# Two banks of the last layer's modulation computed on VectorE from transposed weights, ahead of the recurrence instead of inside it

## The chip, the cores and the metric

The kernel runs on one core of a Trainium2 chip, in fp32, as one program. The metric is the device time of one execution in microseconds; of several runs the median is taken.

## What is computed

The reference chains two blocks over 256 tokens (and 256 context tokens) of 1024 features. The second block has two layers: an even mixer (latent attention and a convolution) and an odd mixer (an RWKV recurrence and neighbourhood attention), each followed by a mixture of 16 experts. Each layer is steered by a vector of 6 x 1024 modulations, computed from one conditioning row `c`:

```python
def second_block(x, c, ctx, c_ctx, ada_w, ada_b, ...):
    for i in range(DEPTH):                       # DEPTH = 2
        mod = jnp.einsum('bd,de->be', jax.nn.silu(c), ada_w[i]) + ada_b[i]   # 1024 x 6144 weights
        mod_c = jax.nn.silu(c_ctx) @ ada_w[i] + ada_b[i]
        sh1, sc1, g1, sh2, sc2, g2 = jnp.split(mod[:, None, :], 6, -1)
        h = rms_norm_2(x, norm1_g[i]) * (1.0 + sc1) + sh1
        ...
        y, yc = odd_mixer(h, hc, ...)            # i = 1: u = h @ w_in, then the recurrence
        x = x + g1 * y
        h = rms_norm_2(x, norm2_g[i]) * (1.0 + sc2) + sh2
        x = x + g2 * expert_choice_ffn(h, ...)
```

For the last layer only `mod` of `c` is used after the first norm (the context's columns count only in `sh1` and `sc1`).

## The kernel before

The program runs stage after stage; engines overlap within a stage and at its edges, in the order in which the program was scheduled. The stages that matter here, with their start in the trace: the first layer's experts (to about 1861 us); `odd_in` (1861 to 2034 us), which norms the tokens, multiplies them by the odd mixer's input weights `od_w_in` and prepares the recurrence; `rwkv` (2034 to 2268 us); the rest of the odd mixer (to 2345 us); the second layer's experts (to the end).

**The products of `odd_in`.** `features` norms and transposes the tokens and splits them into a high and a low part (`ah`, `al`; `al` is written by DVE, L364). A block of 1 MB of `od_w_in` is loaded by the SP queue (L380) into the tile `w`, of which there are three; its two halves are split likewise, `wh` by ACT (L347) and `wl` by DVE (L350), and a `w` is free again when both halves are split. A product is three matmuls (`wh` by `ah`, `wl` by `ah`, `wh` by `al`) for each of eight parts of the depth. `by_features` makes blocks of transposed products: `lwa`, `k`, `sgs` (the values) with 512 columns, `r` and `lg` with 256; each block is evacuated by one ACT and two DVE instructions (L1739, L1741), which shift and add. Then `lengths` norms the keys (a sum on PE, a RECIPROCAL on DVE at L1803, four products with `kk` at L1808), the values are transposed, `low_rank` runs, and the loop over `NO` makes the neighbourhood attention's queries, keys and values from three more sets of weights (`by_pairs`, `by_tokens`). `rwkv` comes behind all that: its first instruction on PE is a product into `py`.

**The modulations.** They are computed in three banks of 2048 columns by a generator, `mods_steps`. One step handles 128 rows of the weights: four loads of 256 KB (`mw`, L550) or one of 1 MB, and four fp32 matmuls with `silu(c)` as the 128x32 stationary operand. `want(m, bank)` allows a bank to be computed, `fill(n)` runs n steps wherever the code calls it, and `need(m, bank)` runs all steps that are still missing. The last layer's bank 0 is computed much earlier. Banks 1 and 2 are handed out inside `rwkv`, two steps at a time (`OF = (2, 2, 2)`): 64 loads `mw` into five buffers and 64 matmuls into `pd` (128 records in the trace, since an fp32 matmul is recorded as two). At the end of a bank the sums are transposed, the bias is added, and for the two gates a row is written out to memory. `by_features`, `by_pairs` and `by_tokens` call `fill(self.rate)` at their end, which in `odd_in` of the kernel before has nothing to run.

**Behind the modulations in `rwkv`.** The recurrence begins with four head pairs b = 0 to 3 (products into `py` and `pg` on PE, exponentials on ACT, products on DVE and POOL). Their triangular blocks `Lx` and `Lc` go to memory (`scr`, L2001) and come back turned round (`fsx<-scr`, L2004) for the substitution, a long run of small DVE instructions (L2018, L2020). The DMAs of both are issued by SP, as are the loads `mw`.

Of the kernel before, what the change touches and what calls it, by code (L numbers as in the profile page):

```python
# [9 lines left out]
F32 = mybir.dt.float32  # L10
# [4 lines left out]
AF = mybir.ActivationFunctionType  # L15
OP = mybir.AluOpType
# [3 lines left out]
D = 1024  # L20
# [65 lines left out]
def lay_out(inp):  # L86
    g = {k: np.asarray(v) for k, v in inp.items()}
    arrays = {}
# [24 lines left out]
    for name in ("w_mod", "ada_w_2", "diff_lambda",  # L113
# [5 lines left out]
    arrays["ctx_2"] = np.ascontiguousarray(g["ctx_2"][0])  # L119
    arrays["xT"] = np.ascontiguousarray(np.concatenate([g["x"][0].T, g["ctx"][0].T], 1).reshape(  # L120
        2, 4, 128, 512).transpose(0, 2, 1, 3))
    arrays["router"] = np.ascontiguousarray(
        g["moe_router_2"].reshape(2, 8, 128, 16).transpose(2, 0, 1, 3).reshape(128, 256))

# [5 lines left out]
    bias = np.full((8, T, T), -1e30, np.float32)  # L130
# [3 lines left out]
    col, qk = Pack(), []  # L134
# [47 lines left out]
    row, colm = (tok // 64).astype(np.float64), (tok % 64).astype(np.float64)  # L182
# [16 lines left out]
    cs = np.cos(2 * np.pi * (np.outer(tok, tok) % T) / T) / 16  # L199
# [18 lines left out]
    p = np.arange(128)  # L218
# [30 lines left out]
class Kernel:  # L249
# [245 lines left out]

    def mods(self, w, l, b, cx, cc, name):

        m = dict(name=name, done=-1, limit=-1)
        m["row"] = [self.dram.tile([2, D], F32, name=f"modr{name}{i}") for i in range(2)]
        self.fillers.append((m, self.mods_steps(m, w[l], f"{b}{l}", cx, cc)))  # L500
        return m

    def mods_steps(self, m, w, b, cx, cc):
        nc = self.nc
        for c in ("col", "col1"):
            m[c] = self.keep.tile([128, 12, 4, 2], F32, name=f"mod{c}{m['name'][1]}", bufs=1)
        sl = self.small.tile([128, KT, 32], F32, name="sil", bufs=1)
        nc.vector.memset(sl, 0.0)
        for v, cn in enumerate((cx, cc)):
            o, n = self.col_at[cn]  # L510
            nc.scalar.activation(sl[:, :, v], self.cols[:, o:o + n], AF.Silu)
        o, _ = self.col_at[b]
        for bank in range(3):
            ps = self.psum(self.modtag)
            for k in range(KT):
                ws = self.mod_weights(w[k * 128:(k + 1) * 128, bank * 2048:(bank + 1) * 2048])
                for g in range(4):
                    self.mm(ps[32 * g:32 * g + 32, :], sl[:, k, :], ws[g] if self.modpool else ws[:, g * 512:(g + 1) * 512],
                            k == 0, k == KT - 1)
                if k < KT - 1:  # L520
                    yield
            mr = self.small.tile([128, 512], F32, name="modrow", bufs=1)
            nc.scalar.copy(mr, ps)
            pt = self.psum()
            for s in range(4):
                self.transpose(pt[:, s * 128:(s + 1) * 128], mr[:, s * 128:(s + 1) * 128])
            v = pt.rearrange("p (s g r) -> p s g r", s=4, g=4)
            cs = slice(bank * 4, bank * 4 + 4)
            bias = self.cols[:, o + 16 * bank:o + 16 * bank + 16].rearrange("p (s g) -> p s g", s=4)
            c = m["col"][:, cs]  # L530
            nc.vector.tensor_tensor(c, v[:, :, :, 0:2], bias[:, :, :, None].to_broadcast([128, 4, 4, 2]), OP.add)
            nc.vector.tensor_scalar(m["col1"][:, cs], c, 1.0, None, OP.add)
            for sec, bk, g0 in ((0, 1, 0), (1, 2, 2)):
                if bk == bank:
                    gc = self.small.tile([128, 2, 2, 4], F32, name="gatec", bufs=1)
                    nc.vector.tensor_copy(gc, c[:, :, g0:g0 + 2].rearrange("p s g v -> p v g s"))
                    pt = self.psum()[:16, :128]
                    self.transpose(pt, gc.rearrange("p v g s -> p (v g s)"))
                    mr = self.small.tile([128, 512], F32, name="modrow", bufs=1)[:16, :128]
                    nc.scalar.copy(mr, pt)  # L540
                    nc.scalar.dma_start(m["row"][sec].rearrange("v (k f) -> (v k) f", f=128), mr)
            m["done"] = bank
            yield

    def mod_weights(self, src):

        if self.modpool:
            ws = [self.modpool() for _ in range(4)]
            for g, wt in enumerate(ws):
                self.nc.sync.dma_start(wt, src[:, g * 512:(g + 1) * 512])  # L550
            return ws
        wt = self.raw((1, 2048))[:, 0]
        self.last_load = self.nc.sync.dma_start(wt, src)
        return wt
# [53 lines left out]
class Block1(Kernel):  # L608
# [77 lines left out]
    def block1(self, mods):  # L686
        with self.pool("w4", "right") as self.fourth:
            self.need(mods[0], 0)
            for l in range(2):
                self.layer1(l, mods[l])  # L690
        self.fourth = None
# [961 lines left out]
class Odd(Moe):  # L1653
# [55 lines left out]
    def odd_in(self, m, od):  # L1709

        nc, a = self.nc, self.a
        W = lambda c0: a["od_w_in_2"][0, c0]
        with self.dense():
            self.need(m, 0)
            tmp = self.tmp
            self.wide = WIDE
            G = self.affine(m, "n1g1", 1, "G1")
            ah = tmp.tile([128, KT, 512], F32R, name="ah", bufs=1)
# [50 lines left out]
            self.nv = od.tile([128, 4, 512], F32, name="nv", bufs=1)  # L1769
            gain = self.small.tile([128, 1], F32, name="nag", bufs=1)  # L1770
            nc.vector.tensor_scalar(gain, self.col("nag", 0), self.col("nag", 1), 0.125, OP.mult, OP.mult)
            for c0, n, dT in NO:
                if dT is None:
                    self.by_tokens(self.halves(a["od_w_in_2"], c0), ahs, als, range(4),
                                   lambda tb, ps: nc.scalar.copy(self.nv[:, tb], ps))
                    continue
                dT = self.nkT if n == 4 else self.nqT
                for j in range(2):
                    z = tmp.tile([128, 4, 256], F32, name="nz", bufs=2)[:, :n]
                    self.by_pairs(W(c0 + j * 256), ahs, als, range(n // 2),  # L1780
                                   lambda tp, ps: nc.scalar.copy(z[:, tp * 2:tp * 2 + 2], ps))
                    self.head_norm(z.rearrange("p t (h d) -> p (t h) d", h=4), 64)
                    for i in range(2):
                        ps = self.psum()
                        for tb in range(n):
                            self.transpose(ps[:, tb * 128:(tb + 1) * 128], z[:, tb, i * 128:(i + 1) * 128])
                        nc.scalar.activation(dT[:, 2 * j + i], ps[:, :n * 128], AF.Copy, scale=gain if n == 2 else 1.0)
# [487 lines left out]
```

## Time and profile before

| | us |
|---|---|
| median of 3 runs | 2809.76 (2806.86 to 2818.59) |
| profiled execution | 2814.77 |
| its span in the trace | 2813.0 |

| engine | busy us | share of the span |
|---|---|---|
| PE (matmul) | 2558.9 | 91% |
| DVE | 1184.1 | 42% |
| ACT | 771.4 | 27% |
| POOL | 303.9 | 11% |

The shares are averages over stages with different limits, so they tell little of one change. In the two expert stages the DMA engines run at 407 to 421 GB/s and set the pace; in the stages between them PE, DVE or a chain over several engines does. The mean granted clock of TensorE over the run is 0.96 of full speed.

### The profile page before, as it was taken

How to read it: one execution, taken by the hardware profiler on the slowest of the kernel's cores; microseconds unless marked ns; L12 is line 12 of the kernel's file. 1: busy time of each engine (PE TensorE's matmuls, PEld its weight loads, DVE VectorE, ACT ScalarE, POOL GpSimd, SP SyncE). 2: the span in 40 equal slices, each digit the busy share in tenths (PEclk: the TensorE clock that was granted, in tenths of full speed). 3: DMA queues.
4: the chain of work that ended last, by engine and by line, in shares of the span. 5: the costliest groups of instructions: out<-in, count | busy, mean ns of one | idle time of the engine just before them, and what ended most of it. 6: DMA issues, size and time to landing. Idle time of an engine off the chain costs nothing.

```text
span 2813.0 us, 34600 instructions
## 1 busy us (share of the span) xinstructions
PE 2558.9 (91%) x13867; PEld 1564.3 (56%) x13867; DVE 1184.1 (42%) x2273; ACT 771.4 (27%) x1394; POOL 303.9 (11%) x370
## 2 busy tenths in 40 slices
PE   7999899997998998989899999989996897888887
PEld 4667688885766796757633333348644684222121
DVE  3355633347456467997511111155449452000000
ACT  3242322223343343276410000033442432000000
POOL 0001400004102003300100000000023130000000
PEclk8999999998998999999999999999998998999999
DMA  7443623223456854242699999953185548999998
GB/s 307 150 165 119 225 90 105 90 101 126 161 199 252 301 181 173 70 169 81 262 404 421 421 421 421 421 229 110 37 243 135 162 169 350 415 421 421 421 421 347
DMA packets 147216, 683.42 MB, mean 243 GB/s; under 512 B 38384, under 2 KB 51568, under 8 KB 71920
## 3 DMA queue, kind: packets, MB, share of 16 engines
q1 hardware_dynamic: 140656, 663.91, 61.6%
q10 hardware_dynamic: 6400, 17.31, 2.0%
q8 instruction: 109, 1.79, 0.3%
q14 instruction: 51, 0.42, 0.0%
HBM read 667.73 MB, written 11.60 MB: 241 GB/s over the span
## 4 chain that ended last, share of the span: by engine, by line
PE 51%; DMA 26%; DVE 8%; issue 2%; ACT 2%; POOL 0%; SPq 0%; ACTq 0%; DVEq 0%; POOLq 0%
DMA w<-in_moe_w 24%; PE pd L327 19%; PE pS L327 12%; PE pt L327 6%; PE pu L327 5%; PE ps L327 2%; PE pg L327 2%; PE pm L327 2%; DVE al L364 1%; PE ps L472 1%; PE pt L472 1%; PE pO L327 1%; DVE fs L2018 1%; DVE co L1152 1%; PE py L327 1%
## 5 line engine op out<-in xcount | busy, mean ns | idle before, releaser
L327 PE MATMUL pu<-w,xs 128*64 128x512 f32 (+1 forms) x2040 | 494.4, 599 | 42.9 <-DMA w<-in_moe_w 42.9
L350 DVE TENSOR_TENSOR wl<-w,wh 128x1024 fp32r<-128x1024 f32 x229 | 285.4, 1249 | 346.4 <-ACT wh L347 345.8
L347 ACT CAST wh<-w 128x1024 fp32r<-128x1024 f32 x250 | 259.7, 1041 | 598.5 <-PE pd L327 272.8
L327 PEld LDWEIGHTS pu<-w,xs 128*64 128x64 f32 (+1 forms) x2040 | 149.6, 123 | 370.7 <-issue 255.2
L327 PE MATMUL pd<-w,hidT 128*64 128x512 f32 (+1 forms) x1024 | 253.6, 598 | 31.0 <-DMA w<-in_moe_w 30.2
L327 PE MATMUL pd<-ah,wh 128*128 128x512 f32 (+2 forms) x656 | 233.6, 361 | 7.8 <-ACT wh L347 3.5
L327 PE MATMUL pd<-al,wh 128*128 128x512 f32 (+2 forms) x656 | 232.1, 355 | 8.6 <-DVE al L364 8.6
L327 PE MATMUL pd<-ah,wl 128*128 128x512 f32 (+1 forms) x648 | 227.1, 352 | 0.0
L1606 DVE TENSOR_TENSOR hid<-hid,pu 128x512 f32<-128x512 f32 x24 | 16.5, 688 | 439.3 <-PE pu L327 439.3
L1605 ACT ACTIVATE hid<-pu 128x512 f32<-128x512 f32 x24 | 14.2, 597 | 677.5 <-PE pu L327 677.5
L327 PEld LDWEIGHTS pd<-w,hidT 128*64 128x64 f32 (+1 forms) x1024 | 74.8, 122 | 200.2 <-issue 116.0
L327 PEld LDWEIGHTS pd<-ah,wh 128*128 128x128 f32 (+1 forms) x656 | 127.8, 196 | 42.6 <-issue 15.8
L327 PEld LDWEIGHTS pd<-al,wh 128*128 128x128 f32 (+1 forms) x656 | 128.6, 196 | 30.0 <-DVE al L364 10.5
L327 PE MATMUL pm<-w,sil 128*32 128x512 f32 x640 | 105.3, 697 | 41.9 <-DMA w<-in_w_mod 26.3
L327 PEld LDWEIGHTS pd<-ah,wl 128*128 128x128 f32 x648 | 126.9, 196 | 22.6 <-issue 8.2
L1615 DVE TENSOR_TENSOR ys<-pd,g 128x512 f32<-128x512 f32 x24 | 16.6, 692 | 285.0 <-PE pd L327 285.0
L1152 DVE SCALAR_TENSOR_TENSOR co<-cv,cols,co 128x512 f32<-128x512 f32 x120 | 100.5, 862 | 0.4
L1625 DVE TENSOR_TENSOR X<-X,ps 128x512 f32<-128x512 f32 x80 | 54.8, 687 | 107.2 <-PE ps L327 107.2
L327 PE MATMUL pS<-al,wh 128*128 128x256 f32 (+1 forms) x264 | 90.0, 342 | 5.0 <-DVE al L364 5.0
L327 PE MATMUL pS<-ah,wh 128*128 128x256 f32 (+1 forms) x264 | 89.8, 341 | 1.4 <-ACT ah L363 1.3
L327 PE MATMUL pS<-ah,wl 128*128 128x256 f32 (+1 forms) x264 | 89.3, 338 | 0.0
L327 PE MATMUL ps<-ys,gt 128*128 128x512 f32 x160 | 81.9, 625 | 2.1 <-DVE X L1625 2.1
(593 smaller groups left out, 4416.0 us busy)
## 6 DMA issues: line engine op xcount, KB each, us to landing
w<-in_moe_w SPq DMA_DIRECT2D x383, 1024.0 KB, 19.8
w<-in_w_mod SPq DMA_DIRECT2D x48, 1024.0 KB, 5.1
w<-in_w_up SPq DMA_DIRECT2D x32, 1024.0 KB, 4.9
w<-in_w_down SPq DMA_DIRECT2D x32, 1024.0 KB, 4.9
w<-in_ada_w SPq DMA_DIRECT2D x32, 1024.0 KB, 5.0
w<-in_w_in SPq DMA_DIRECT2D x20, 1024.0 KB, 4.9
mw<-in_ada_w SPq DMA_DIRECT2D x64, 256.0 KB, 3.9
w<-in_od_w_in SPq DMA_DIRECT2D x13, 1024.0 KB, 4.9
```

Of the source, the lines that this page charges most:

```text
L327: ins = self.nc.tensor.matmul(out, lhsT, rhs, start=start, stop=stop, skip_group_check=True)
L347: nc.scalar.copy(h, src)
L350: (le or nc.vector).tensor_tensor(l, src, h.bitcast(F32), OP.subtract)
L364: nc.vector.tensor_tensor(l, t, h.bitcast(F32), OP.subtract)
L472: ins = self.nc.tensor.transpose(out, in_, self.ident[:rows, :rows])
L1152: nc.vector.scalar_tensor_tensor(y, CV[:, f, :, t:t + T], self.col(f"dw{t}", f), y, OP.mult, OP.add)
L1605: nc.scalar.activation(hid[:, cs], up["moe_w1_2"][c], AF.Silu)
L1606: nc.vector.tensor_tensor(hid[:, cs], hid[:, cs], up["moe_w3_2"][c], OP.mult)
L1615: nc.vector.tensor_tensor(ys[:, cs], down[c], gate[:, cs], OP.mult)
L1625: nc.vector.tensor_tensor(self.X[tb][:, cs], self.X[tb][:, cs], ps, OP.add)
L2018: nc.vector.tensor_tensor(t, LM[:, s, tr, None].to_broadcast([128, nt_, nj]), X[:, s, None, jr].to_broadcast([128, nt_, nj]), OP.mult)
```

## The change

Banks 1 and 2 of the last layer no longer go to PE. `odd_in` gives the modulations room (a tile `sx` for the row `silu(c)`, broadcast to 128 partitions) and allows bank 2; every `fill` at the end of a step in `odd_in` then runs one step of a new generator, `mods_by_dve`. A step loads 1 MB of weights that were transposed on the host (`modT`) into the ring `w` of the input products, and runs two DVE instructions (128x1024, a pair in what follows) that multiply by `sx` and sum along the row into one column of `modacc`. A bank has eight steps. `need(m, 2)` just ahead of the loop over `NO` runs what is left. The order of the additions changes, the values computed do not.

```diff
+    arrays["modT"] = ... w[1][:, 2048:].T ... reshape(2, 4, 2, 2, 128, 1024).transpose(0, 1, 2, 4, 3, 5)
+    arrays["crow"] = np.stack([g[n].reshape(-1) for n in ("c", "c_2")])
@@ mods_steps
         for bank in range(3):
+            if m["room"] is not None and bank:
+                yield from self.mods_by_dve(m, bank, o)
+                continue
             ps = self.psum(self.modtag)
@@
+    def mods_by_dve(self, m, bank, o):
+        nc = self.nc
+        pair = "ma".index(m["name"][0])
+        if bank == 1:
+            m["sx"] = m["room"]()
+            nc.scalar.dma_start(m["sx"], self.a["crow"][pair:pair + 1].to_broadcast([128, D]))
+            nc.scalar.activation(m["sx"], m["sx"], AF.Silu)
+        cs = slice(bank * 4, bank * 4 + 4)
+        c = m["col"][:, cs]
+        nc.gpsimd.memset(c, 0.0)
+        acc = self.small.tile([128, 4, 4], F32, name="modacc", bufs=1)
+        for g in range(4):
+            for h in range(2):
+                wt = self.raw((2, 1024))
+                self.last_load = nc.sync.dma_start(wt, self.a["modT"][pair, bank - 1, g, h])
+                for i in range(2):
+                    nc.vector.scalar_tensor_tensor(wt[:, i], wt[:, i], 1.0, m["sx"], OP.mult, OP.mult,
+                                                   accum_out=acc[:, 2 * h + i, g:g + 1])
+                if g + h < 4:
+                    yield
+        bias = self.cols[:, o + 16 * bank:o + 16 * bank + 16].rearrange("p (s g) -> p s g", s=4)
+        nc.vector.tensor_tensor(c[:, :, :, 0], acc, bias, OP.add)
+        nc.vector.tensor_scalar(m["col1"][:, cs], c, 1.0, None, OP.add)
+        self.gate_rows(m, bank, c)          # the gate's row, as before
+        m["done"] = bank
+        yield
@@ odd_in
             tmp = self.tmp
+            m["room"] = lambda: tmp.tile([128, D], F32, name="sx", bufs=1)
+            self.want(m, 2)
@@
+            self.need(m, 2)
             for c0, n, dT in NO:
```

The program is scheduled anew, so the order on the engines moves too. Lines of the kernel after stand higher than the same lines before: L575 is the new DVE instruction, L573 its load, L355 the split L350, L385 the load L380, L1666 the sum L1625, L489 to L494 the steps L484 to L489.

DVE, at the end of the first layer's experts (`X`) and the start of `features` (`rsw`, `xrs`: the norm's reciprocal root), before:

```order
L1625 TENSOR_TENSOR X_74<-X_74,ps 128x512 x2
L484 TENSOR_SCALAR rsw<-ss 128x1
L485 TENSOR_SCALAR xrs<-rsw 128x1
L488 TENSOR_SCALAR rsw<-xrs,rsw 128x1
L489 TENSOR_SCALAR xrs<-rsw,xrs 128x1
```

and after:

```order
L1666 TENSOR_TENSOR X_74<-X_74,ps 128x512 x2
L575 SCALAR_TENSOR_TENSOR w,modacc<-w,sx 128x1024 x2
L489 TENSOR_SCALAR rsw<-ss 128x1 x2
L575 SCALAR_TENSOR_TENSOR w,modacc<-w,sx 128x1024 x2
L490 TENSOR_SCALAR xrs<-rsw 128x1 x2
L493 TENSOR_SCALAR rsw<-xrs,rsw 128x1 x2
L494 TENSOR_SCALAR xrs<-rsw,xrs 128x1 x2
```

Two pairs now stand ahead of the norm that every input product waits for; a third stands 29 rows below the second, between the two scalings `nk<-X` of the same stage.

DVE, from the last block of `by_features` (`lg`) over `lengths` to the first weights of `NO` (the `wl` behind `kk`), before:

```order
L350 TENSOR_TENSOR wl<-w,wh 128x1024
L1739 SCALAR_TENSOR_TENSOR lg<-pS,cols,lg 128x255
L1741 SCALAR_TENSOR_TENSOR lg<-pS,cols,lg 128x255
L1802 TENSOR_SCALAR tf<-ps 8x512
L1803 RECIPROCAL tf<-tf 8x512
L1808 TENSOR_TENSOR kk<-kk,ps 128x512 x2
L350 TENSOR_TENSOR wl<-w,wh 128x1024
```

and after:

```order
L1782 SCALAR_TENSOR_TENSOR lg<-pS,cols,lg 128x255
L575 SCALAR_TENSOR_TENSOR w,modacc<-w,sx 128x1024 x2
L1784 SCALAR_TENSOR_TENSOR lg<-pS,cols,lg 128x255
L1846 TENSOR_SCALAR tf<-ps 8x512
L575 SCALAR_TENSOR_TENSOR w,modacc<-w,sx 128x1024 x2
L1847 RECIPROCAL tf<-tf 8x512
L575 SCALAR_TENSOR_TENSOR w,modacc<-w,sx 128x1024 x6
L1852 TENSOR_TENSOR kk<-kk,ps 128x512 x2
L575 SCALAR_TENSOR_TENSOR w,modacc<-w,sx 128x1024 x2
L1852 TENSOR_TENSOR kk<-kk,ps 128x512
L580 TENSOR_TENSOR modcol_9263<-modacc,cols 128x16
L355 TENSOR_TENSOR wl<-w,wh 128x1024
```

Six of bank 2's eight pairs stand here, ahead of the first weights of `NO` (the last `wl` shown); the other two stand 2 and 6 rows ahead of the first row shown. In the kernel before three `wl` of `NO` stand ahead of the `lg` rows, of which the first row shown is the third.

SP, the loads of the input weights up to `NO` (the last but one of `by_features`, the last, then six of `NO`) and the recurrence's first DMAs, before:

```order
L380 DMA w<-in_od_w_in 128x1024
L380 DMA w<-in_od_w_in 128x2048 x6
L550 DMA mw<-in_ada_w 128x512 x19
L1978 DMA sp_13924<-MV 128x4x128
L1989 DMA sp_13924<-zt 64x4x128 x2
L550 DMA mw<-in_ada_w 128x512 x2
```

and after:

```order
L573 DMA w<-in_modT 128x2048
L385 DMA w<-in_od_w_in 128x1024
L573 DMA w<-in_modT 128x2048 x9
L385 DMA w<-in_od_w_in 128x2048 x6
L1885 DMA nbias<-in_na_bias 128x512
L2022 DMA sp_14013<-MV 128x4x128
L2033 DMA sp_14013<-zt 64x4x128 x4
```

All loads of the transposed weights stand ahead of the first load of `NO`, and all of them share the three tiles `w`; the recurrence's own DMAs no longer have loads `mw` between them. The first load of `NO` takes the tile that the third pair from the last has read, and the two loads behind it those of the last two pairs.

## Rows read from the trace of the kernel before

**Rows 1.** Engines by stage, whole core (x: instructions; PEclk: granted clock).

```profile
core 0: us, PE busy (x) PEld busy (x) DVE busy (x) ACT busy (x) POOL busy (x), PEclk, DMA share, GB/s
...
1860.00:1890.00 30.00, 22.43 (x90) 16.89 (x89) 18.70 (x62) 14.61 (x33) 0.00 (x0) 0.77 0.29 107
1890.00:1947.00 57.00, 57.00 (x308) 49.27 (x308) 36.40 (x46) 24.14 (x33) 0.00 (x0) 1.00 0.35 122
1947.00:2033.00 86.00, 79.61 (x456) 61.63 (x453) 40.15 (x80) 37.63 (x58) 2.38 (x3) 0.97 0.16 55
2033.00:2060.00 27.00, 25.05 (x247) 11.74 (x248) 13.79 (x21) 11.12 (x32) 10.88 (x12) 0.89 0.61 183
2060.00:2090.00 30.00, 30.00 (x223) 11.06 (x222) 15.32 (x28) 15.43 (x33) 6.81 (x9) 1.00 0.79 227
2090.00:2130.00 40.00, 31.91 (x325) 14.89 (x324) 28.40 (x57) 17.75 (x51) 19.87 (x20) 1.00 0.71 214
2130.00:2180.00 50.00, 29.71 (x520) 23.92 (x521) 47.15 (x126) 9.02 (x19) 9.63 (x8) 0.73 0.58 128
```

**Rows 2.** Stage table for instructions touching tile `mw` alone.

```profile
2033.00:2060.00 27.00, 13.76 (x39) 2.03 (x40) 0.89 0.61 183
2060.00:2090.00 30.00, 14.06 (x42) 1.85 (x41) 1.00 0.79 227
```

**Rows 3.** Tile `mw`, its SP loads (issue time min/median/max).

```profile
L550 SPq DMA_DIRECT2D mw<-in_ada_w x64: 327/382/1917, 2018.3 to 2122.3; - x64
```

**Rows 4.** VectorE instructions by form, whole run (count, busy, mean ns, idle before).

```profile
L350 DVE TENSOR_TENSOR wl<-w,wh 128x1024 fp32r<-128x1024 f32 x229 | 285.4, 1249 | 346.4 <-ACT wh L347 345.8
...
L1916 DVE TENSOR_TENSOR Bh<-Bh,iin 128x512 f32<-128x512 f32 x8 | 9.2, 1156 | 0.0
...
L639 DVE SCALAR_TENSOR_TENSOR X<-X,bmv,gb 128x1024 f32<-128x1024 f32 x2 | 2.6, 1278 | 0.0
```

**Rows 5.** VectorE's timeline in `features` (start us, length us, idle before).

```profile
1861.63 0.14 DVE L484 TENSOR_SCALAR rsw<-ss 128x1 f32<-128x1 f32 x1
...
1864.22 0.74 DVE L993 TENSOR_SCALAR nv<-X,xrs 128x1024 f32<-128x1024 f32 x1
...
1871.63 0.75 DVE L993 TENSOR_SCALAR nk<-X,xrs 128x1024 f32<-128x1024 f32 x1
...
1883.99 0.43 DVE L364 TENSOR_TENSOR al<-tf,ah 128x256 fp32r<-128x256 f32 x1 [0.48 <-ACT ah L363]
```

**Rows 6.** VectorE's timeline from the last blocks of `by_features` on.

```profile
1947.54 1.23 DVE L350 TENSOR_TENSOR wl<-w,wh 128x1024 fp32r<-128x1024 f32 x1 [0.74 <-ACT wh L347]
...
1949.19 0.48 DVE L1741 SCALAR_TENSOR_TENSOR lg<-pS,cols,lg 128x255 f32<-128x255 f32 x1
...
1953.14 3.34 DVE L1803 RECIPROCAL tf<-tf 8x512 f32<-8x512 f32 x1
```

**Rows 7.** Chain that ended last, `NO` and the recurrence's front (start us, us).

```profile
1949.21 2.23 PE pt L327 x17
1951.44 0.95 PE ps L327 x2
...
2033.63 2.08 PE py L327 x8
...
2040.68 5.40 DMA mw<-in_ada_w
...
2051.06 4.04 DMA mw<-in_ada_w
...
2091.37 2.55 DMA scr<-Lc
2093.98 6.03 DMA fsx<-scr
```

**Rows 8.** Page, part 6: loads of the odd mixer's weights.

```profile
w<-in_od_w_in SPq DMA_DIRECT2D x13, 1024.0 KB, 4.9
```

**Rows 9.** Waits from 2033 to 2100 us (us in total, times, longest).

```profile
ACT MV L1972 <- PE py L327: 16.6, 5, 8.2
```

More of the change, by code (lines that the diff above doesn't have):

```diff
@@ L121, in lay_out @@
         2, 4, 128, 512).transpose(0, 2, 1, 3))
+    arrays["modT"] = np.ascontiguousarray(np.stack(
+        [np.asarray(g[n][1])[:, 2048:].T.reshape(2, 4, 2, 2, 128, 1024).transpose(0, 1, 2, 4, 3, 5)
+         for n in ("w_mod", "ada_w_2")]))
+    arrays["crow"] = np.ascontiguousarray(np.stack([g[n].reshape(-1) for n in ("c", "c_2")]))
     arrays["router"] = np.ascontiguousarray(
@@ L496, in mods @@
     def mods(self, w, l, b, cx, cc, name):
-        m = dict(name=name, done=-1, limit=-1)
+        m = dict(name=name, done=-1, limit=-1, room=None)
         m["row"] = [self.dram.tile([2, D], F32, name=f"modr{name}{i}") for i in range(2)]
@@ L532, in mods_steps @@
             nc.vector.tensor_scalar(m["col1"][:, cs], c, 1.0, None, OP.add)
[L533 to L541, printed above, removed]
+            self.gate_rows(m, bank, c)
@@ L542, in mods_steps, with gate_rows @@
             m["done"] = bank
             yield
+    def gate_rows(self, m, bank, c):
+        nc = self.nc
+        for sec, bk, g0 in ((0, 1, 0), (1, 2, 2)):
+            if bk == bank:
+                gc = self.small.tile([128, 2, 2, 4], F32, name="gatec", bufs=1)
+                nc.vector.tensor_copy(gc, c[:, :, g0:g0 + 2].rearrange("p s g v -> p v g s"))
+                pt = self.psum()[:16, :128]
+                self.transpose(pt, gc.rearrange("p v g s -> p (v g s)"))
+                mr = self.small.tile([128, 512], F32, name="modrow", bufs=1)[:16, :128]
+                nc.scalar.copy(mr, pt)
+                nc.scalar.dma_start(m["row"][sec].rearrange("v (k f) -> (v k) f", f=128), mr)
@@ new lines, in mods_by_dve @@
+    def mods_by_dve(self, m, bank, o):
+        nc = self.nc
+        pair = "ma".index(m["name"][0])
[19 more added lines that the diff above has]
+        nc.vector.tensor_scalar(m["col1"][:, cs], c, 1.0, None, OP.add)
+        self.gate_rows(m, bank, c)
+        m["done"] = bank
+        yield
```

## The prediction

> **What bounds the kernel now.** I read the table of the stages first, since the shares of the whole run say nothing of this change [rows 1]. It shows four different limits in a row. From 1860 to 1890 us no engine is full: the norm and the splits go from hand to hand, PE is busy 22.4 of 30 us and its granted clock falls to 0.77. From 1890 to 1947 PE is busy all 57 us, DVE 36.4. From 1947 to 2033 PE is busy 79.6 of 86. Then comes the stretch that the change wants to relieve, 2033 to 2090: PE is busy 55.05 of 57 us, and the table for the modulations' tile alone shows that 13.76 + 14.06 = 27.8 us of that are the matmuls on `mw` [rows 2]. From 2130 to 2180 DVE is the limit (47.15 of 50). The chain that ended last agrees: through 2033 to 2090 it lies on PE, with two waits for loads of `mw` (5.40 and 4.04 us) in it; at 2091 it leaves PE for the DMAs of `Lc` and of `fsx`, 2.55 and 6.03 us [rows 7]. So the matmuls on `mw` are on the path in the recurrence's front, and behind 2100 they lie under DVE. Loads `mw` go out until 2122.3 [rows 3]; those of the last 20 us cost nothing.
>
> **What is taken away.** The front is 57 us of which 27.8 are the modulations. The rest of PE's work there is 55.05 - 27.8 = 27.2 us; DVE has 13.79 + 15.32 = 29.1, ACT 26.6, POOL 17.7 [rows 1]. The best end: the front shrinks to the busiest engine left, 29, a gain of 28. The worst end: PE and DVE work strictly by turns, 27.2 + 29.1 = 56.3, a gain of nothing. The waits say that the engines do hand on to each other (ACT waited 16.6 us for products of PE here) [rows 9], but part of that is PE being busy with `mw`. The nearest stretch of handovers without modulations is 1860 to 1890, where the busiest engine fills 22.43 of 30 us, 75% [rows 1]. At that share 29.1 us of DVE take 39 us; I add 2 for the lower clock of a PE with pauses (0.77 there, 0.89 and 1.00 here). So the front takes 41 and the gain is 16. The turned blocks come back a little faster, since SP no longer has loads `mw` to issue between them and the DMA share was 0.71 to 0.79: of 2.55 + 6.03 us I take 1.5, between 0 and 3. Together 17.5, between 0 and 31. Behind that DVE's work up to 2180 is unchanged, and it simply starts earlier.
>
> **What a pair costs.** 32 DVE instructions of 128x1024 are added, in 16 pairs. No row shows one with a running sum. The nearest is a SCALAR_TENSOR_TENSOR of the same size with two fp32 operands from SBUF, 1278 ns; the split `wl` of that size takes 1249; the slowest of DVE's products over long rows is `Bh<-Bh,iin`, 1156 ns for 512, which would be 2.3 us for 1024 [rows 4]. I take 1.3 us, by the row of the same operation and size, so 2.6 us a pair; the ends are 2.45 and 4.6.
> The row of 1278 ns shows no loss from two fp32 operands. The Trainium skill's Vector Engine (DVE) Microarchitecture Reference, Points that are easy to get wrong, speaks against the change: this operation with two sources in SBUF that aren't bf16 runs at half the rate, as no read port is left for the accumulator. No run here has such a sum; by that rule a pair would be 5.1 us, and the sum below would be 31 us longer, about 2845.
>
> **Three pairs in `features`.** Two stand ahead of the norm's small steps and a third between the scalings of `nk`. DVE goes from `rsw` at 1861.63 to the last `al` at 1883.99 with few pauses, and that `al` is what the first full product needs [rows 5]. 3 x 2.6 = 7.8 us; in 30 us DVE is idle for 11.3, so some is absorbed late, by pauses for ACT such as the 0.48 ahead of the last `al`. I take 6.5, between 4 and 8. Their loads need no wait: the first has a free tile and the second is issued when the first split is done, some 4 us earlier than DVE wants it (a load lands in 4.9 us [rows 8]).
>
> **Five pairs under `by_features`.** 36.4 + 5 x 2.6 = 49.4 us of DVE in 57 us of PE [rows 1]: they are hidden by the products, as the change says. The tiles are shared, one load of weights and one of `modT` by turns, and 5 us of landing fit twice into the time of two blocks. Cost 0; without that cover it would be 13.
>
> **Eight pairs of bank 2.** Here the cover ends. Six of the eight stand behind the last blocks on DVE, and the first weights of `NO` are loaded into the tile that the sixth pair frees, and are split only behind the eighth. PE has nothing else: the transposes of the values and `low_rank`, which it could do, stand behind the first product of `NO` in its order. Before, `wl` for `NO` was split at 1947.54 and the first product began at 1949.21 [rows 6, 7]. After: the last `lg` step, at 1949.19 before, moves by 6.5 to about 1956.2 at its end. Then come pair three (2.6), a step on `tf` (0.7), pair four (2.6), the RECIPROCAL (3.34 [rows 6]), pairs five and six (5.2): 1970.6. The load follows, 4.9 us [rows 8], and the split by ACT and DVE, some 2 us: the first product at about 1977.5, 28 us later than before (6.5 of it is the delay of `features`). Pairs seven and eight and the steps on `kk` end by 1978, at the same time. Of the 28, PE wins back the four products of `lengths`, 0.95 us each [rows 7], which now lie in its pause, and some 2 of the 6.4 us in which it idled between 1947 and 2033. A clock that falls in a pause of 20 us may cost 0 to 2. So the recurrence's first product, at 2033.63 before [rows 7], starts 22 us later, between 16 and 27.
>
> **Edits without cost.** The row `sx` (512 KB) and its one ACT step lie in the tail of the experts; at most 1 us. The gate rows and their transposes only move. POOL's two memsets wait for nothing. SP's loads of constants and of the saved `X` move behind a `modT` load by some 8 us, and are read later than that. The bytes are the same, 16 MB.
>
> **The sum.** +22 - 17.5 = +4.5 us. On the profiled execution, 2814.77, that is 2819.3; its time stands 5.0 above the median of the runs, so for the median I forecast 2809.76 + 4.5 = 2814.3, say 2814. With the bounds of the two large terms: 16 - 31 = -15 to 27 - 0 = +27.
>
> **Rivals.** (1) PE alone made the front long. Then all 28 us come back, and 3 behind: 22 - 31 = -9, and -15 if the start moves by only 16: 2795 to 2801. For it: PE is 97% busy and on the chain throughout [rows 1, 7]. Against: DVE has 29.1 us to do and gets its operands from PE. (2) Slower: the matmuls on `mw` filled pauses that stay. The front is then a chain from PE to ACT, DVE and POOL, and only some 7 us come back: +15, 2825. It decides when less than 8 us come back. For it: the waits of ACT for PE [rows 9]. Against: the two waits for `mw` on the chain, 9.4 us in all [rows 7]. (3) The running sum makes DVE's instruction as slow as the row of 2.3 us for 1024: 2 us more per pair, 6 in `features`, 1 in `by_features` (36.4 + 23 is over 57), 16 in bank 2: +23.5, 2838. The page named above says about that. (4) The change does what it says, and all sums lie under products: the start moves only by the 6.5 of `features`, 6.5 - 17.5 = -11, 2799. Against it stands the order: the first load of `NO` waits for a pair that comes behind the last products.
>
> **How the numbers follow.** A measurement of this kernel can tell some 0.5%, 14 us, from no change. Forecast 0.47 (2805 to 2823), rival 1 0.18, rival 2 0.20, rival 3 0.09, rival 4 0.06. Under 2795.7 lie half of rival 1 and a third of rival 4 at their ends, and little of the forecast: 0.13. Over 2823.8 lie two thirds of rival 2, rival 3 and the forecast's upper tail: 0.27. The rest, 0.60, is within 0.5%. The range from 2796 to 2836 leaves out rival 3's upper half and the lower ends of rivals 1 and 4.
>
> **What would show it.** The mean of L575 (1.3 us or 2.3); PE's first product of `NO` (1949.2 before, 1977 expected); the first product into `py` (2033.6 before, 2056 expected); the time from there to the landing of `fsx` (66.4 us before, 49 expected). I am wrong if PE's pause ahead of `NO` is under 12 us or the front takes less than 35 or more than 50.

## The result

The kernel after takes 2828.3 us (median of 9 runs, 2819.86 to 2840.36), the kernel before 2810.75 (9 runs, 2806.86 to 2819.23): a ratio of 1.006, with a 95% interval from 1.0047 to 1.0074, so 13 to 21 us slower. The forecast was 2814 with a range of 2796 to 2836. The time lies in the range, on the side that was forecast, but the loss is about four times the 4.5 us of the sum, and it is over the bound of 0.5%, to which I had given 0.27.

The profiled execution of after took 2840.36 us (span 2838.6), 12 us over its median, that of before 4 us over its own. So stages are compared below, and totals by medians and ratios.

Groups of the new instruction in after (count | busy us, mean ns of one | idle before):

```profile
L575 DVE SCALAR_TENSOR_TENSOR w<-w,sx 128x1024 f32<-128x1024 f32 x32 | 37.6, 1215 | 4.4 <-DMA w<-in_modT 4.3
...
L575 DVE DVE_READ_ACCUMULATOR w<-w,sx 128x1 f32 x32 | 2.5, 80 | 0.0
```

One of the new sums takes 1.22 us and the reading of the accumulator behind it runs into the next: they follow at 1.145 us (1861.00, 1862.14, 1863.29), 2.3 us a pair. That is close to the price of the nearest row in [rows 4] (2.6 us for two) and a little under my lower end of 2.45. The halved rate of which the Trainium skill warns (Vector Engine (DVE) Microarchitecture Reference, Points that are easy to get wrong) isn't there: with two fp32 sources in SBUF and an accumulator the instruction takes no longer than the 1278 ns of `X<-X,bmv,gb` without one.

VectorE's timeline of after, at the places of [rows 5, 6]:

```profile
1861.00 1.22 DVE L575 SCALAR_TENSOR_TENSOR w<-w,sx 128x1024 f32<-128x1024 f32 x1
...
1867.73 0.74 DVE L1034 TENSOR_SCALAR nv<-X,xrs 128x1024 f32<-128x1024 f32 x1
...
1889.46 0.43 DVE L369 TENSOR_TENSOR al<-tf,ah 128x256 fp32r<-128x256 f32 x1 [0.48 <-ACT ah L368]
...
1961.80 3.33 DVE L1847 RECIPROCAL tf<-tf 8x512 f32<-8x512 f32 x1
...
1976.36 1.23 DVE L355 TENSOR_TENSOR wl<-w,wh 128x1024 fp32r<-128x1024 f32 x1 [0.24 <-ACT wh L352]
```

The first pair starts 0.6 us ahead of where `rsw` stood, the scaling `nv` comes at 1867.7 instead of 1864.2, and the last `al` at 1889.46 instead of 1883.99. The first weights of `NO` (`wl`) are split at 1976.4. The chain that ended last in after, at the places of [rows 7]:

```profile
1972.60 3.78 PE ps L332 x4
1976.38 0.58 PE pt L332
...
2057.07 0.52 ACT tri L1913
...
2097.12 3.77 PE py L332 x4
...
2101.96 3.71 PE py L332 x4
...
2108.54 2.84 DMA scr<-Lc
2111.44 4.29 DMA fsx<-scr
```

The first product of `NO` begins at 1976.38, where 1977.5 was forecast (1949.21 before). It does so behind the last products of `lengths` (`ps`, from 1972.60); the load of its weights, on which the forecast went, and their split by ACT end at the same time to 0.1 us, and in the second trace of after (e5_after_again below) the chain goes through that load. The `tri` copy ahead of the recurrence's first product is at 2057.1, and that product at 2057.9 (2033.6 before). The stage table of after, as in [rows 1]:

```profile
1896.00:1956.00 60.00, 59.88 (x314) 49.53 (x312) 49.50 (x76) 22.43 (x32) 0.00 (x0) 1.00 0.60 215
1956.00:1976.00 20.00, 7.18 (x8) 2.32 (x8) 20.00 (x32) 4.33 (x5) 0.00 (x0) 0.58 0.92 338
1976.00:2058.00 82.00, 74.22 (x443) 61.43 (x442) 36.19 (x81) 36.08 (x55) 2.32 (x3) 0.94 0.17 60
2058.00:2088.00 30.00, 22.98 (x330) 18.70 (x332) 16.75 (x28) 13.45 (x39) 13.83 (x14) 0.65 0.15 41
2088.00:2115.00 27.00, 21.00 (x150) 10.47 (x144) 10.76 (x18) 13.25 (x27) 6.93 (x9) 0.65 0.30 67
2115.00:2195.00 80.00, 40.98 (x544) 33.85 (x544) 74.22 (x173) 21.53 (x59) 26.77 (x24) 0.61 0.35 89
2195.00:2228.00 33.00, 31.43 (x413) 23.37 (x415) 10.53 (x23) 10.77 (x22) 1.80 (x1) 0.54 0.44 105
```

Under `by_features` PE is busy 59.88 of 60 us: the five pairs are hidden. From 1956 to 1976 it works 7.18 of 20 us, at a granted clock of 0.58. Then the recurrence: where [rows 1] has 0.89 and 1.00 at its front, after has 0.65 and 0.65, and it stays at 0.61 and 0.54 up to 2228, the level of 1.2 GHz most of the time.

### The profile page after: what moved, and what is told of

Its sections match the earlier page's. It is cut to its first block, busy times and chain, and to the rows that moved or that the text cites. A ratio compares the mean times of both kernels' runs of the same rounds, so it can differ in the third digit from the quotient of the medians.

```text
span 2838.6 us, 34302 instructions
## 1 busy us (share of the span) xinstructions
PE 2549.1 (90%) x13731; PEld 1579.2 (56%) x13731; DVE 1220.1 (43%) x2337; ACT 770.7 (27%) x1393; POOL 303.1 (11%) x372
## 4 chain that ended last, share of the span: by engine, by line
PE 49%; DMA 27%; DVE 9%; ACT 2%; issue 2%; POOL 0%; SPq 0%; ACTq 0%; DVEq 0%; POOLq 0%
DMA w<-in_moe_w 23%; PE pd L332 17%; PE pS L332 11%; PE pu L332 6%; PE pt L332 5%; PE pg L332 3%; PE ps L332 2%; PE pm L332 2%; DMA w<-in_modT 1%; PE ps L477 1%; DMA w<-in_ada_w 1%; DVE w L575 1%; DVE al L369 1%; PE pt L477 1%; DVE fs L2062 1%
## 5 line engine op out<-in xcount | busy, mean ns | idle before, releaser
L355 DVE TENSOR_TENSOR wl<-w,wh 128x1024 fp32r<-128x1024 f32 x229 | 285.4, 1248 | 331.9 <-ACT wh L352 331.5
L1666 DVE TENSOR_TENSOR X<-X,ps 128x512 f32<-128x512 f32 x80 | 54.8, 687 | 107.3 <-PE ps L332 107.3
```

The lines of the kernel that those rows point to most:

```text
L355: (le or nc.vector).tensor_tensor(l, src, h.bitcast(F32), OP.subtract)
L1666: nc.vector.tensor_tensor(self.X[tb][:, cs], self.X[tb][:, cs], ps, OP.add)
```

## Where the time went

Five starts can be read in every trace's timelines: the end of the last sum `X` of the experts, the first product into `py`, the first step `fs` of the first substitution, the write-out of the second substitution (`scr<-sgs`), and the first load `mv` of the recurrence's end. Between them, in us, with the clock granted from about 30 to 57 us behind the first `py`, and each kernel's ratio to the kernel before:

| kernel | X to py | py to fs (the front) | clock | scr<-sgs to mv | ratio (95%) |
|---|---|---|---|---|---|
| before | 171.9 | 66.4 | 1.00 | 26.2 | 1 |
| after | 196.8 | 57.8 | 0.65 | 33.4 | 1.0060 (1.0047 to 1.0074) |
| e5_after_again | 197.6 | 55.2 | 0.61 | 34.9 | 1.0044 (1.0026 to 1.0061) |
| e1_no_sums | 181.4 | 55.9 | 0.62 | 33.6 | 0.9987 (0.9972 to 1.0003) |
| e2_no_sums_fill | 181.6 | 53.9 | 0.81 | 26.6 | 0.9973 (0.9955 to 0.9991) |
| e3_held | 191.8 | 55.6 | 0.60 | 34.9 | 1.0021 (1.0003 to 1.0039) |
| e4_late | 185.6 | 58.1 | 0.64 | 34.9 | 1.0015 (0.9996 to 1.0035) |
| e6_late_held | 179.9 | 58.3 | 0.64 | 33.4 | 1.0007 (0.9991 to 1.0022) |
| e7_late_held_fill | 179.3 | 55.5 | 0.81 | 23.3 | 0.9972 (0.9955 to 0.9990) |
| e8_bank1_held | 174.6 | 59.8 | 1.00 | 26.0 | 0.9954 (0.9937 to 0.9970) |
| e9_after_fill | 195.9 | 56.3 | 0.85 | 25.8 | 1.0034 (1.0016 to 1.0052) |
| e10_bank1_behind | 171.7 | 54.7 | 0.65 | 34.9 | 0.9988 (0.9970 to 1.0007) |
| e11_bank1_fill | 171.7 | 60.5 | 1.00 | 25.9 | 0.9975 (0.9952 to 0.9997) |
| e12_after_order | 197.6 | 55.6 | 0.61 | 25.4 | 1.0055 (1.0035 to 1.0076) |

Each trace is of one execution, and two stages vary between executions of one program: from `mv` to the output weights 66.1 us in after and 74.4 in e5_after_again, and from the first load of the last experts' weights (`w<-in_moe_w`) to the end 515 and 518 us in the traces of before and after and 505 to 510 in those of all the others. No reading below rests on those. By the table after starts the recurrence 25 us later, gets 9 to 11 back in its front, and loses 7 to 9 again at the wait ahead of `mv`, which the prediction doesn't mention. That adds up to 23 or 24 us. The profiled executions differ by 25.6 and 21.4, the medians by 0.60% and 0.44%, 17 and 12 us: the steps have the size of one execution each, and no trace here shows where the faster ones save.

## The experiments

Two theories went in. Theory 1 is the prediction's: taking the matmuls on `mw` out of the front is worth 17.5 us. Theory 2 came from the stage table of after: without them TensorE's granted clock falls, and its own products take back what was gained.

**Removal alone, and removal with other work for PE.** The loads and sums are left out:

```diff
-            m["sx"] = m["room"]() ... (its load and its silu)
+        nc.gpsimd.memset(acc, 0.0)
...
-                wt = self.raw((2, 1024)) ... (the load and the two sums)
```

> The kernel after without the 16 loads of transposed weights, without the row sx and without the 32 sums on DVE (the two banks then hold the bias alone), so neither PE nor DVE computes the two banks: what the removal from the recurrence brings by itself. Theory 1 (as predicted: the front of the recurrence is shortened by 16 and the turned blocks return 1.5 us sooner): 17.5 us under the kernel before, about 2793, and 49 us from the first product into py to the landing of fsx. Theory 2 (without the matmuls on mw TensorE is granted the lower of its two levels for much of the recurrence's front and up to the substitution's end, and its own products there take nearly twice as long): 58 us to the landing, the granted clock from the first product into py on for 60 us at 0.7 or less, and only 0 to 8 us under the kernel before, 2803 to 2811.

Measured: 2811.08 us against 2815.55 on the same chip, ratio 0.9987, front 55.9 us, clock 0.62, wait 33.6 us. So in this order computing the two banks nowhere at all is worth 0 to 8 us. Theory 2's numbers hold, and the front is far from the 49 us of theory 1. The total by itself doesn't decide, since part of it is an accident: PE waits 5.4 and 5.0 us for two last norms of `NO` (`nz`), one behind the other, where it waits so long once in before, and the recurrence starts 9.4 us later behind the first product of `NO` than in before. Without that the removal would be worth some 13 us (an estimate, 9 to 17), and the longer wait ahead of `mv` hides more.

```diff
         def fill(n):
             with self.later(OLATE, "pS"):
                 self.fill(n)
+                ps = self.psum(self.modtag)
+                for _ in range(4):
+                    self.mm(ps, tri[:, :128], tri, True, True)
```

> As e1_no_sums, with four extra fp32r matmuls of 128x128 by 512 columns on resident data (the results are read by nobody, nothing is loaded for them) at each of the twelve places where the recurrence handed out modulation steps, 48 in all. Theory 1: the clock doesn't matter there, the extra matmuls cost nothing or their own time, about 10 us at the most: 0 to 10 us over e1_no_sums. Theory 2: the clock granted in the front rises to 0.9 or more, the front gets shorter or stays as it is although PE has more to do (50 to 56 us to the landing of fsx), and the whole is 2 to 8 us under e1_no_sums.

Measured: ratio 0.9973, clock 0.81, front 53.9 us, wait 26.6 us. With more work PE has the shorter front and the shorter wait, as theory 2 said; in the total the two intervals overlap.

**The same on after itself.** The three added lines alone, beside a second look at after:

> The kernel after as it is, beside the variants below on one chip. 1.004 to 1.008 of the kernel before. In its trace: the first product of NO 18 us behind the last step on lg, 56 to 59 us from the first product into py to the start of the substitution.

> The kernel after with nothing changed but the 48 extra fp32r matmuls in the recurrence's front (results read by nobody). Theory 2: the granted clock of the front rises from 0.65 to 0.8 or more, the front is 1 to 3 us shorter, the wait ahead of mv falls from 34 to 24 to 28 us, and the whole is 8 to 14 us under after: 1.000 to 1.002 of before. Theory 1 (no part of the clock): 0 to 10 us over after, 1.005 to 1.009.

Measured: 1.0044 for after, 1.0034 with the extra matmuls; 2828.5 and 2824.3 us. The stage table of e9_after_fill for the front:

```profile
2061.00:2091.00 30.00, 27.06 (x342) 20.83 (x344) 16.52 (x28) 13.13 (x39) 14.06 (x14) 0.86 0.14 37
2091.00:2118.00 27.00, 22.42 (x215) 12.86 (x214) 11.73 (x21) 14.71 (x30) 7.07 (x9) 0.85 0.38 88
```

The clock is 0.86 and 0.85 instead of 0.65. Groups of PE from 2030 to 2130 us, first before, then after, then e9_after_fill (busy us, mean ns of one):

```profile
L327 PE MATMUL py<-V,MN 64*64 64x64 f32 x192 | 7.3, 222 | 0.1
...
L327 PE MATMUL py<-low,lwa 64*128 64x512 f32 x8 | 4.5, 641 | 0.0
L327 PE MATMUL py<-lwa,low 64*128 64x512 f32 x8 | 4.4, 628 | 0.0
```

```profile
L332 PE MATMUL py<-V,MN 64*64 64x64 f32 x192 | 11.4, 297 | 9.3 <-DVE MN L2003 9.3
...
L332 PE MATMUL py<-lwa,low 64*128 64x512 f32 x8 | 7.6, 1097 | 0.2 <-DVE sg L1867 0.2
L332 PE MATMUL py<-low,lwa 64*128 64x512 f32 x8 | 6.0, 869 | 2.1 <-DVE sg L1867 1.6 <-ACT iin L1952 0.4
```

```profile
L332 PE MATMUL pd<-tri 128*128 128x512 f32 x48 | 15.8, 450 | 0.0
...
L332 PE MATMUL py<-lwa,low 64*128 64x512 f32 x8 | 6.0, 869 | 0.5 <-DVE sg L1867 0.4
...
L332 PE MATMUL py<-low,lwa 64*128 64x512 f32 x8 | 4.2, 628 | 0.0
```

In after the same 208 instructions take 25.0 us where they took 16.2. That is the price of the low clock on PE in these three groups, 8.8 us; in the chain above two pairs of `lwa,low` stand with 3.77 and 3.71 us. With the extra matmuls `low,lwa` is back at 628 ns, `lwa,low`, later, half way at 869. But the front is 56.3 us, no shorter than the 55.2 and 57.8 of after: 15.8 us of added work and a faster PE cancel. The total, 8 to 14 us less as expected by theory 2, isn't there either: 0.1% against e5_after_again and 0.26% against the first runs of after, and the intervals overlap in both. So the clock falls and PE pays for it, but it doesn't explain by itself why the front is 56 us and not 49.

**The stall and the delay ahead of the products.**

```diff
+            m["one"] = self.small.tile([128, 1], F32, name="one", bufs=1)
+            nc.vector.tensor_scalar(m["one"], al[:, KT - 1, 511:512].bitcast(F32), 0.0, 1.0, OP.mult, OP.add)
...
-            nc.scalar.activation(m["sx"], m["sx"], AF.Silu)
+            nc.scalar.activation(m["sx"], m["sx"], AF.Silu, scale=m["one"])
```

> The kernel after, with the row sx made dependent on the last al of the features stage, so that no pair of sums stands on DVE ahead of the norm or the splits. Both theories: the delay of the first input product goes (4 to 8 us, 5.5 in the trace of after by the last al), so 2820 to 2824 where after gave 2828. If those pairs cost nothing after all: 2828.

Measured: the recurrence starts 5.7 us sooner than in e5_after_again (191.8 against 197.6), ratio 1.0021. The delay by the three pairs is real and of the forecast size.

```diff
-            self.need(m, 2)
             for c0, n, dT in NO:
                 ...
+            self.need(m, 2)
```

> The kernel after with the call that forces all of bank 2 moved from ahead of the NO loop to behind it, so that one step of bank 2 goes between two blocks of NO, as in by_features. If the stall of PE ahead of NO is what costs: the first product of NO begins at about 1957 instead of 1976, the recurrence 12 to 18 us sooner than in after, 2810 to 2816. If the loads and pairs only move their cost into the loop, by the three shared tiles: 2822 to 2828.

Measured: 12.0 us sooner (185.6), ratio 1.0015. The pause is gone (the first product of `NO` at 1954.3, 22 us sooner), and some 10 us of it come back as a longer loop (92.3 us from there to the first `py`, 81.5 and 82.7 in the two traces of after). Both together:

> Both moves of e3_held and e4_late together: no pair ahead of the splits, and bank 2's pairs between the blocks of NO. If their gains add: the recurrence starts 5 to 9 us later than in the kernel before (24 later in after) and its front is 8 to 10 us shorter, but the wait between the second substitution and the first mv stays 7 us longer (33 to 35 us against 26) by the low clock: 1.000 to 1.003 of before. If the clock had no part in it, 0.994 to 0.998.

Measured: 179.9, ratio 1.0007: the gains add (17.7), and nothing is left of the loss, but nothing is won. The wait is 33.4 us, as expected; whether the clock makes it, as was expected too, comes further down. With the extra matmuls:

> e6_late_held with the 48 extra fp32r matmuls of e2_no_sums_fill in the recurrence's front (their results are read by nobody). Theory 2 (clock): the front is granted 0.8 to 0.9 instead of 0.65 to 0.7, it is 1 to 4 us shorter in spite of 10 us of added products, the wait ahead of mv shrinks to 26 to 29 us; 3 to 10 us under e6_late_held, 0.997 to 1.000 of before. Theory 1: 0 to 10 us over e6_late_held.

Measured: ratio 0.9972, 0.35% under e6_late_held, front 55.5 against 58.3 us, wait 23.3 against 33.4. This is the one pair in which extra matmuls show in the total, and most of it is the wait.

**Half the change.** Bank 2 stays on PE in the recurrence:

```diff
-            if m["room"] is not None and bank:
+            if m["room"] is not None and bank == 1:
...
-            self.want(m, 2)
+            self.want(m, 1)
...
-            self.need(m, 2)
             for c0, n, dT in NO:
```

and `sx` is held back as in e3_held.

> Only bank 1 is summed on DVE, under by_features and not ahead of the splits; bank 2 stays on PE in the recurrence (32 of the 64 loads mw and of their matmuls). Theory 2: the matmuls that stay hold the granted clock of the front at 0.8 or more; the recurrence starts 3 to 6 us later than before, its front is 6 to 10 us shorter, the wait ahead of mv is 26 to 29 us: 0.996 to 1.000 of before. If half the matmuls are too few for the clock: front and wait as in after, 1.000 to 1.003.

Measured: 2801.69 us, ratio 0.9954: faster than both kernels. The front:

```profile
2034.00:2064.00 30.00, 28.09 (x283) 12.82 (x284) 15.94 (x26) 11.96 (x35) 11.26 (x12) 0.92 0.65 201
2064.00:2091.00 27.00, 26.75 (x291) 13.13 (x289) 14.23 (x26) 16.06 (x33) 8.78 (x10) 1.00 0.54 149
```

PE is busy and at full clock as in before. Half of the matmuls taken away give 6.6 us of front (59.8 against 66.4), both halves 8.6 to 11.2. The first half costs 2.7 us ahead of the recurrence (174.6 against 171.9); the second costs 17 more where it stands ahead of `NO` (191.8 in e3_held) and 5 between its blocks (179.9 in e6_late_held).

> e8_bank1_held, whose front was granted 0.92 and 1.00, with the 48 extra matmuls too. With the clock up already they can only cost: 3 to 10 us over e8_bank1_held in the front, 0.997 to 1.000. If extra matmuls help for another reason than the clock: under e8_bank1_held, 0.993 or less.

Measured: ratio 0.9975, front 60.5 us, wait 25.9. Where the clock is up the extra matmuls bring nothing, as expected. In the front they cost 0.7 us (60.5 against 59.8), not the 3 to 10 expected; the 0.2% in the total isn't resolved.

**The wait ahead of `mv`.** In e2, e7, e8, e9 and e11 the front's clock was high and the wait short. So bank 2's matmuls of e8_bank1_held were moved behind the front: no steps are handed out in it, and `silu(c)` depends on the last block `Lc`:

```diff
-OLATE, OF = 2000, (2, 2, 2)
+OLATE, OF = 2000, (0, 2, 2)
...
+        one = self.small.tile([128, 1], F32, name="one", bufs=1)
+        nc.vector.tensor_scalar(one, st[0]["Lc"][:, 0, 3, 0, 0:1], 0.0, 1.0, OP.mult, OP.add)
+        nc.vector.tensor_scalar(m["sil"], m["sil"], one, None, OP.mult)
```

> As e8_bank1_held, but the 32 matmuls of bank 2 wait for the last block Lc of the first four head pairs, so they run behind the front instead of in it. If the granted clock follows what PE does just before: the front runs at 0.6 to 0.7 as in after and is 55 to 58 us (59.8 in e8_bank1_held), the stretch behind it is granted 0.7 or more instead of 0.51, and the wait ahead of mv is 23 to 28 us; the whole within 3 us of e8_bank1_held, 0.994 to 0.997. If it is the low clock in the front itself that leaves work over for later: the wait ahead of mv is 32 to 35 us as in after, 0.998 to 1.000.

Measured: ratio 0.9988, front 54.7 us, wait 34.9. Its stage table:

```profile
2034.00:2064.00 30.00, 22.66 (x339) 17.80 (x340) 18.73 (x32) 15.43 (x47) 15.97 (x17) 0.76 0.20 55
2064.00:2091.00 27.00, 21.71 (x144) 9.06 (x142) 11.95 (x27) 10.35 (x17) 4.80 (x6) 0.65 0.33 80
2091.00:2171.00 80.00, 48.40 (x605) 28.54 (x603) 73.40 (x170) 22.90 (x62) 27.77 (x24) 0.88 0.61 171
2171.00:2204.00 33.00, 32.03 (x372) 23.05 (x372) 9.71 (x21) 10.37 (x21) 1.80 (x1) 0.50 0.43 105
```

The clock did what was expected up to 2171, 0.65 in the front and 0.88 behind it; the wait didn't shrink. But the run doesn't rule out the clock: in the stretch of the wait itself, the last row, it is 0.50, with PE busy 32.03 of 33 us. Another cause had not been looked at, the order. Without matmuls in the front the scheduler had placed the last head pair's product `MN` behind the second substitution on VectorE, in after and in every kernel with the long wait. Timelines of all engines around it, before and then after (start us, length us, idle before):

```profile
2171.04 0.42 DVE L1959 TENSOR_TENSOR MN<-pg,cst 128x256 f32<-128x256 f32 x1
...
2174.55 2.40 PE L327 MATMUL pg<-fsx,Lx 64*64 64x32 f32 x64
...
2179.16 0.34 SPq L2022 DMA_DIRECT2D scr<-sgs  x1
```

```profile
2195.05 0.34 SPq L2066 DMA_DIRECT2D scr<-sgs  x1
...
2196.00 0.42 DVE L2003 TENSOR_TENSOR MN<-pg,cst 128x256 f32<-128x256 f32 x1
...
2199.51 0.32 PE L332 MATMUL pg<-fsx,Lx 64*64 64x32 f32 x2
```

In the order on PE the first triangular products `fsx,Lx`, whose loads were issued by 2178 in after, stand behind the products of that `MN`; they begin 4.6 us ahead of the write-out of the second substitution in before and 4.5 us behind it in after. From there to `mv` it is much the same, 30.8 and 29.0 us, but not for the same reason. This is the stretch from `fsx,Lx` to `mv` in before, after, e8_bank1_held and e7_late_held_fill:

```profile
2174.55:2205.35 30.80, 21.39 (x415) 16.20 (x414) 13.82 (x35) 9.68 (x20) 1.81 (x1) 0.77 0.48 108
2199.51:2228.50 28.99, 28.99 (x415) 21.30 (x414) 9.28 (x20) 10.12 (x20) 1.38 (x1) 0.55 0.39 78
2169.68:2198.60 28.92, 28.92 (x415) 21.23 (x414) 12.74 (x32) 10.04 (x20) 1.80 (x1) 0.55 0.48 115
2175.04:2196.10 21.06, 19.50 (x415) 14.61 (x414) 9.15 (x20) 9.60 (x20) 1.80 (x1) 0.90 0.60 136
```

In after PE is busy throughout at 0.55, and the chain that ended last lies on it; in before PE has pauses, and the chain goes through the DMAs that bring the second substitution's result back:

```profile
2180.25 4.76 DMA scr<-sgs
...
2191.21 4.22 DMA sgs<-scr
```

With the early start the low clock costs nothing here: in e8_bank1_held `fsx,Lx` begins 2.9 us ahead of the write-out, PE is as slow as in after, and the wait is 26.0 us. With a high clock a late start costs nothing either: in e7_late_held_fill `fsx,Lx` begins 2.3 us behind the write-out, but at 0.90 the same work takes 21.1 us, and the wait is 23.3. The long wait stands where both come together: in all seven traces that have it `fsx,Lx` begins 4.5 us behind the write-out, and the stretch runs at 0.50 to 0.55.

In the last run `MN` was brought forward by a dependency, with nothing added on PE:

```diff
+            if d and b == 3:
+                S["one"] = ... (1.0, made from MV[:, 3, 127:128])
...
+                if d and i == 24:
+                    nc.vector.tensor_scalar(t, t, st[d]["one"], None, OP.mult)
...
-        with self.later(SUB1, "pS"):
-            substitute(1)
         for b in range(4):
             spill(1, b)
             fill(OF[2])
+        with self.later(SUB1, "pS"):
+            substitute(1)
```

(The sums `MV`, from which `one` is made, are computed in `spill`, so that now stands ahead of the substitution.)

> The kernel after, with the 25th step of the second substitution made dependent on the last head pair's sums MV, so that the product MN of that pair stands 17 rows ahead of the substitution's last row on DVE (one row behind it in after, 24 ahead of it in the kernel before); nothing is added on PE, so the recurrence's front keeps its low clock. Order theory (PE takes its work in order, and the first triangular products stand behind that pair's products): those products begin 1 to 4 us ahead of the substitution's end instead of 4.5 us behind it, the wait from there to the first mv falls from 33 to 35 us to 25 to 29 us, the front stays at 55 to 58 us and about 0.65; 2 to 8 us under after, 1.001 to 1.004 of before (the dependency itself may cost DVE 1 to 3 us). Clock theory: the wait stays at 33 to 35 us, 1.004 to 1.007.

```profile
2190.24 1.01 DVE L2003 TENSOR_TENSOR MN<-pg,cst 128x512 f32<-128x512 f32 x2
...
2195.36 2.06 PE L332 MATMUL pg<-fsx,Lx 64*64 64x32 f32 x64
...
2198.59 0.56 SPq L2071 DMA_DIRECT2D scr<-sgs  x1
```

Measured: `fsx,Lx` begins 3.2 us ahead of the write-out, the wait is 25.4 us, and the front is as in after, 55.6 us at 0.61. So the order alone takes the wait away: `fsx,Lx` begins 7.7 us sooner against the write-out than in after, and the wait is 8.0 us shorter. (The clock in the stretch rose too, to 0.73, but e8_bank1_held shows the short wait at 0.55.) The total doesn't show it: 1.0055, where after had 1.0060 and 1.0044 and 1.001 to 1.004 was expected. The dependency made the second substitution 4 to 5 us longer (32.2 us from one write-out to the other, 27.7 and 28.4 in the two traces of after), and the 4 to 6 us that remain are less than the intervals resolve.

## Why the prediction came out as it did

- **What bounds the kernel.** Right: the matmuls on `mw` lay on the path of the front, and half of them taken away made a faster kernel.
- **What a pair costs.** 2.3 us where 2.6 was taken. The row of the same operation and size was the right one to take; rival 3 is out.
- **Three pairs in `features`.** 5.5 us by the last `al`, 5.7 by e3_held, forecast 6.5. Right.
- **Five pairs under `by_features`.** Hidden, as forecast.
- **Eight pairs of bank 2.** Right nearly to the us: the first product of `NO` at 1976.38, forecast 1977.5; the recurrence 24 to 25 us later, forecast 22. PE won back less than I took. From the first product of `NO` to the first `py` it was busy 73.75 of 81.5 us, where it was busy 77.47 of 84.5 before: its work fell by 3.7 us, the size forecast for the products of `lengths`, but it idled 7.8 us instead of 7.0, where I had counted on 2 less.
- **What is taken away.** This term failed, and with it the sum: 17.5 forecast, 8.6 to 11.2 measured from the first `py` to the first `fs`. The step was the length that is left, 41 us: I took DVE as the busiest engine left, at the share of 75% borrowed from 1860 to 1890 (39 us), and 2 us for the clock. From the first `py` to the issue of `Lc` it took 48.9 and 46.9 us in the two traces of after:

```profile
2057.91:2106.82 48.91, 39.61 (x398) 25.40 (x400) 27.21 (x46) 24.51 (x60) 17.60 (x20) 0.64 0.18 44
2058.08:2105.01 46.93, 37.35 (x398) 23.70 (x400) 27.14 (x46) 24.47 (x60) 17.61 (x20) 0.68 0.18 46
```

The busiest engine left is PE, with 39.6 and 37.4 us where I counted 27.2 for it, at a clock of 0.64 and 0.68; DVE fills 56 and 58%, not 75%. So the 2 us for the clock were too few: PE's own work grew by 10 to 12. How the missing 6 to 8 us divide between the clock and the handovers stays open: no run had a front without added work and at full clock. The 1.5 us for the turned blocks was right (10.1 us before, 8.9 and 8.3 after from the issue of `Lc` to `fs`). To the landing of `fsx` the front took 57.8 and 55.2 us, over the 50 that I had named as a sign of being wrong.
- **Behind the front, "it simply starts earlier".** Wrong, and no term of the sum: 7 to 9 us were lost at the wait ahead of `mv`, by an order that the change moved some 140 us behind the start of the recurrence, together with the low clock there. The rows of both orders were to be had before the run; I read them only where the change stands.
- **The rivals.** The nearest was rival 2, at 0.20: it decides when less than 8 us come back, and 8.6 less 7.3 is 1.3 in after, 11.2 less 8.7 is 2.5 in e5_after_again. Its price, 2825, is close to 2828, but its reason, pauses that stay, is only a part, so the closeness is in part luck. Rival 3's +23.5 is counted from the forecast of 2814, unlike the others, which count from the kernel before. Rival 1 fell: with PE alone as the limit the front would have lost 28 us.

## What to carry to other kernels

Work taken off an engine is worth the measured length of the stage without it, not its own busy time: leave the work out in one kernel first (here 0 to 8 us of the 45 us of matmuls on `mw`, 10.5 in the front itself), before paying 25 to move it elsewhere. Moved work was free here only under a stage that another engine bounds, up to its last instruction: with the half that fitted under the products the kernel won 0.46% (e8_bank1_held), with the other half ahead of `NO` too it lost 0.21% (e3_held), and with it between the blocks it came out even (e6_late_held). Where a scheduler sets the order, compare the orders of all engines up to the end of the program, since an emptier stage lets it place things otherwise far behind.

## What the runs showed of the hardware

The granted clock doesn't follow the share of time in which PE has work in the records. The last stretch of the table in e5_after_again, and then the same stretch of e11_bank1_fill:

```profile
2195.00:2228.00 33.00, 33.00 (x417) 23.60 (x415) 9.69 (x20) 11.31 (x23) 1.80 (x1) 0.50 0.39 85
```

```profile
2168.00:2201.00 33.00, 29.03 (x488) 22.28 (x488) 14.60 (x36) 12.87 (x26) 1.80 (x1) 0.71 0.51 132
```

PE is busy all of 33 us at 0.50 in the one, and 29.03 us at 0.71 in the other, with much the same products. Nor does the clock of the stretch ahead decide it: that was 0.56 in e5_after_again and 0.77 in e11_bank1_fill, but 0.88 in e10_bank1_behind, whose last row above has PE busy 32.03 of 33 us at 0.50 again. What decides it no run here shows. So 33 us of PE busy in the records can stay at the lower level, 1.2 GHz, and "PE busy" in a stage table can be work at half speed: it has to be read with the clock beside it.

A VectorE sum with an accumulator, 128x1024 in fp32 from two sources in SBUF, costs 1.145 us in a row of them, its reading of the accumulator (80 ns in the records) overlapped.
